# One transformer block on one core: low weight parts on VectorE alone, and two more weight blocks in seven-product form

## The chip, the core and the metric

The kernel runs on one core of a Trainium2 chip. The core has TensorE (PE, with its weight loads PEld), VectorE (DVE), ScalarE (ACT), GpSimd (POOL) and SyncE (SP), each with its own queue that is worked off in order. The metric is the time of one execution on the device in microseconds (us). About 0.5% is what a measurement of this kernel can tell from no change.

## The reference

One layer, a sequence of 512 tokens of width 1024, all in float32. Three sub-layers, each with an RMSNorm before and after, and a residual:

```
proj = rms_norm(x) @ w_in                      # q, k, v for 8 forgetting heads and 8 chunked heads, 8 gates
mix  = [rms(fox_attention), rms(chunk_attention)] @ w_out;   x += rms_norm(mix)
ca   = softmax(h @ w_mem_q @ k_mem.T / 16) @ v_mem @ w_mem_o;  x += rms_norm(ca)     # k_mem, v_mem from mem @ w_mem_kv
h    = rms_norm(x)
g, u = split(h @ w_gate_up)                    # 1024 x 5632
x   += rms_norm((silu(g) * u) @ w_down)        # 2816 x 1024
```

## The kernel before

**Three products for one.** TensorE works on fp32r, a shortened float32. To keep the precision of float32, every operand is split into a high part (the value rounded to fp32r, written by ScalarE) and a low part (the value less its high part). `mm3` issues three matmuls for one product: high by high, high by low, low by high (lines 147 to 149).

**Weights of the first two sub-layers.** `load_unit` (from line 105) brings one unit of weights (w_in, w_out, w_mem_kv, w_mem_q, w_mem_o, the first gate and up blocks) in pieces of 512 KB, tile `raw`, three buffers. For each piece ScalarE writes `hi` (line 124). The low part `lo` is shared out: a number `pk` of the piece's k-blocks goes to GpSimd (line 127), the rest to VectorE (line 131). Of units 256 wide the second piece gives three of its four blocks to GpSimd, so VectorE has 128x256 of it and GpSimd 128x768; of units 18 to 21 (512 wide, w_mem_kv) the second piece goes to GpSimd whole, 128x1024. The first piece of each unit is VectorE's alone. In all GpSimd writes 20 low parts, 16 of 128x768 and 4 of 128x1024. GpSimd also computes the norms' inverse roots (`rstd_of`, line 154, a power), masks and squares.

**The feed-forward part.** Its input columns are cut into 22 blocks of 128: even numbers are gate (G), odd ones up (U). Blocks 0 and 1 come from the units above. A block from 2 on is made in one of two ways. By eight products (`eight`): a 2 by 2 block product as written, 8 products of 4 k-blocks, each three matmuls of 256 columns, 96 matmuls. By seven products (`seven`): a Strassen scheme, 84 matmuls, for which VectorE forms four sums of weight quarters (lines 918 to 921) and puts the output together from the products (lines 1078 to 1088):

```
product(p26[:, left], (h[:, 0], l[:, 0]), b21)
dve.tensor_tensor(out=O[:, 0], in0=halves(p26), in1=twice(v), op=ALU.add)                  # L1078
dve.tensor_tensor(out=O[:, 1, 0], in0=p35[:, left], in1=O[:, 0, 1], op=ALU.add)            # L1079
product(p4[:, left], (h[:, 1], l[:, 1]), t4)
((h, l),) = take()
product(p17[:, right], (h[:, 0], l[:, 0]), t3)
...
product(p35[:, right], (h[:, 1], l[:, 1]), t1)
```

The last product writes into `p35`, the PSUM tile that L1079 reads, so it waits for L1079. An up block has two more VectorE instructions, the products with the gate (L1098, L1100). For the output blocks u = 1 to 3 a further split of the result follows (`keep`, L986 and L987). The tuple `EIGHT` names the blocks that are made by eight products: 2, 3, 8, 13 and 18 of 20.

**The ring.** The weights of these blocks lie in `ring_hi` and `ring_lo`: two single slots of 512 columns and three double slots of 1024. A seven-product block has four items (one single, three doubles), an eight-product block two doubles. A slot is filled again when TensorE has used it: DMA into `fraw` (three buffers), ScalarE writes the high part (L891), VectorE the low part (L892), for items made of sums after the sums.

**What sets the order.** The instructions are put in order, engine by engine, by a list scheduler when the program is built, from priorities (`later`) and its own idea of durations. A change of the work on one engine changes the order on all of them. `w_down` (22 items through the same ring) follows, and with it the last norm.

Of the kernel before, what the change touches and what calls it, by code (L numbers as in the profile page):

```python
# [11 lines left out]
ALU = mybir.AluOpType  # L12
# [24 lines left out]
def hybrid_block_kernel(  # L37
# [20 lines left out]
    act, dve, pool, pe = nc.scalar, nc.vector, nc.gpsimd, nc.tensor  # L58
# [12 lines left out]
    def f32(ap):  # L71
        return ap.bitcast(F32)
# [32 lines left out]
    def load_unit(w, k0, nkb, c0, ncol, dst=None, skip=0):  # L105
        u = len(loaded)
        if dst is None:
            def place(name):
                flat = wp.tile([P, KB * 256 + 48], F32R, tag=name, name=f"{name}{u}", bufs=2)
                return flat[:, skip : skip + nkb * ncol].rearrange("p (k n) -> p k n", k=nkb)  # L110

            hi, lo = place("hi"), place("lo")
        else:
            hi, lo = dst()
        step = nkb if nkb * ncol <= 1024 else 4 if ncol < 512 else 2
        j = 0
        for n in [min(step, nkb - k) for k in range(0, nkb, step)]:
            raw = wp.tile([P, n, ncol], F32, tag="raw", name=f"raw{u}_{j}", bufs=3)
            r0 = (k0 + j) * P
            nc.sync.dma_start(  # L120
                raw,
                w[r0 : r0 + n * P, c0 : c0 + ncol].rearrange("(k p) n -> p k n", p=P),
            )
            act.copy(hi[:, j : j + n, :], raw)  # L124
            pk = 0 if j == 0 or not 0 <= u < 24 else 3 if ncol == 256 else 2 if u >= 18 else 0
            if pk:
                pool.tensor_tensor(  # L127
                    out=lo[:, j : j + pk, :], in0=raw[:, :pk, :], in1=f32(hi[:, j : j + pk, :]), op=ALU.subtract
                )
            if pk < n:  # L130
                dve.tensor_tensor(  # L131
                    out=lo[:, j + pk : j + n, :], in0=raw[:, pk:, :], in1=f32(hi[:, j + pk : j + n, :]), op=ALU.subtract
                )
            j += n
        loaded.append((hi, lo))

# [2 lines left out]
    def unit(ahead=1):  # L139
        n = used[0]  # L140
        used[0] += 1
        while len(loaded) < min(n + 1 + ahead, len(units)):
            load_unit(*units[len(loaded)])
        return loaded[n]
# [63 lines left out]
    for side in range(2):  # L208
        for g in fox_order if side == 0 else (0, 1):
            c = (0, 1544)[side] + 256 * g  # L210
            n = 264 if (side, g) == (0, 1) else 256
# [22 lines left out]
    with tc.tile_pool(name="mix", bufs=1, reuse_waits="tile") as bp:  # L234
# [114 lines left out]
        for t in range(NT):  # L349
# [3 lines left out]
                out=z[:, t, :], in0=acc0[t][:, 256:264], scalar=r, in1=gn[:, B_F : B_F + 8],  # L353
# [284 lines left out]
        with later(-5):  # L638
            for half in range(2):
                hi, lo = unit()  # L640
# [10 lines left out]
    with tc.tile_pool(name="cross", bufs=1, reuse_waits="tile") as cp:  # L651
# [20 lines left out]
        with later(-115):  # L672
            for c in range(4):
                hi, lo = unit()
                acc = bank("a")
                for b in range(2):
# [9 lines left out]
                    out=kT[:, 1, 2 * c : 2 * c + 2, :], in0=a3,  # L686
                    in1=f32(kT[:, 0, 2 * c : 2 * c + 2, :]), op=ALU.subtract,
# [4 lines left out]
        for half in range(2):  # L692
            hi, lo = unit()
            for t in range(NT):
                acc = bank("a")
                for k in range(4):
# [4 lines left out]
                    out=m, in0=acc, scalar=rs_g[1][:, t : t + 1], in1=m, op0=ALU.mult, op1=ALU.add  # L701
# [14 lines left out]
        for half in range(2):  # L716
            accs = [bank("a"), bank("a")]
            for k0 in (0, 4):
                hi, lo = unit()
# [17 lines left out]
        for h in range(4):  # L737
            hi, lo = unit()
            q = qq[:, h % 2]
            for b in range(2):  # L740
                acc = bank("a")
                cs = slice(b * P, (b + 1) * P)
                for k in range(KB):
# [3 lines left out]
                    out=q[:, 1, b, :], in0=acc, scalar=1.0 / 16.0, in1=f32(q[:, 0, b, :]),  # L747
# [3 lines left out]
            for i in range(0, NT, 2):  # L751
                s = bank("s")
                for j in range(2):
# [8 lines left out]
                    out=nm, in_=s.rearrange("p (j n) -> p j n", j=2), axis=AX.X, op=ALU.max, negate=True  # L762
# [8 lines left out]
                for j in range(2):  # L771
                    dve.tensor_scalar(
                        out=p[:, i + j, :], in0=p[:, i + j, :], scalar1=rs[:, j : j + 1],
# [11 lines left out]
            for b in range(2):  # L785
                acc = bank("o")
                cs = slice((2 * h + b) * P, (2 * h + b + 1) * P)
                for k in range(2):
# [6 lines left out]
                    out=oTl[2 * h + b], in0=acc, in1=f32(oTh[2 * h + b]), op=ALU.subtract  # L795
# [27 lines left out]
        for pair in range(2):  # L823
            for half, w in enumerate((w0, w1)):
                for t in (2 * pair, 2 * pair + 1):
                    acc = bank("a")
                    ts = slice(t * P, (t + 1) * P)
                    for k in range(KB):
                        hi, lo = w[k // 4]
# [104 lines left out]
                    fill_from(at, dict(k=4, n=256), lambda k0=k0: load_raw(w_gate_up, k0, 4, c0, 256)),  # L934
                )

        EIGHT = (2, 3, 8, 13, 18)
        for n in range(2, FB):
            (eight_weights if n in EIGHT else seven_weights)(n, (n % 2) * FF + (n // 2) * 256)
        for half in range(2):  # L940
# [28 lines left out]
        def hidden(u):  # L969

            if u == 0:
                return G
            if u < 4:
                return U.rearrange("p t b n -> p b t n")
            if u in (4, 8, 10):
                tag, size = {4: ("vm", 4160), 8: ("pt", 2112), 10: ("up", 2176)}[u]
                gf.append(cp.tile([P, size], F32, tag=tag, name=f"gf{u}"))
            at = (u % 4 if u < 8 else u % 2) * 1024
            return gf[-1][:, at : at + 1024].rearrange("p (b t n) -> p b t n", b=2, t=2)
# [43 lines left out]
        def up_eight(dst):  # L1023
            def done(m, acc):
                dve.tensor_tensor(out=dst[:, m], in0=G[:, :, m], in1=halves(acc), op=ALU.mult)

            return done

        def eight(tags, done):
            accs = [bank(tag) for tag in tags]  # L1030
            for half, bs in enumerate(((b11, b12), (b21, b22))):
                ((h, l),) = take()
                for m in range(2):
                    w = [a[:, :, m * P : (m + 1) * P] for a in (h, l)]
                    for n, ns in enumerate((left, right)):
                        product(accs[m][:, ns], w, bs[n], half == 0 and n == 0, half == 1 and n == 1)
                    if half:
                        done(m, accs[m])
# [67 lines left out]
        for u in range(1, FB // 2):  # L1106
            if 2 * u in EIGHT:
                eight(("a", "a"), gate_eight)
            else:
                seven(G, ("a", "a", "a", "o"), gate_seven)  # L1110
            dst = hidden(u)
            if 2 * u + 1 in EIGHT:
                eight(("s", "s"), up_eight(dst))
# [20 lines left out]
        for half, tail in enumerate((2, 3)):  # L1134
# [17 lines left out]
            for t in range(NT):  # L1152
# [8 lines left out]
                else:  # L1161
# [6 lines left out]
                    for hf in range(2):  # L1168
                        c2 = slice(hf * 512, (hf + 1) * 512)
                        dve.scalar_tensor_tensor(  # L1170
                            out=yd[:, t, c2], in0=yd[:, t, c2], scalar=r, in1=xr[:, t, c2],
# [58 lines left out]
```

## Time and profile before

| what | us |
|---|---|
| median of 3 runs | 801.57 (798.55 to 803.13) |
| the profiled execution, its own time | 796.84 |
| its span, first to last instruction | 795.1 |
| PE busy | 769.5 (97%) |
| VectorE busy | 550.0 (69%) |
| ScalarE busy | 407.2 (51%) |
| GpSimd busy | 117.4 (15%) |

The profiled execution is 4.7 us faster than the median of the runs; durations below are its own. A busy PE is not one at its peak, since matmuls overlap: where matmuls follow one another without a stop, the distance of their starts is what one costs. Idle time in brackets is that of the engine just before the instruction, with the instruction that ended it.

### The profile page before, as it was taken

Reading aid. Unit: us, or ns where it says so; the run is one execution under the profiler, and the core shown is the slowest. Engines: PE = TensorE matmul, PEld = TensorE weight load, DVE = VectorE, ACT = ScalarE, POOL = GpSimd, SP = SyncE. Lnnn points to the kernel's source line nnn. Section 1 sums busy time; section 2 is a strip of 40 time slices with the busy share of each in tenths; the row PEclk is TensorE's granted clock in tenths of the full one; section 3 lists DMA queues with packets and bytes.
Section 4 is the critical chain, followed back from the end, with each engine's and each line's share of the span. In section 5 each row is a group of like instructions: output and inputs, shape, how many; then the busy total and the mean of one; then the engine's idle time right before and its main releaser. Section 6 shows DMA issues by size and latency. Waiting matters only on the chain.

```text
span 795.1 us, 12344 instructions
## 1 busy us (share of the span) xinstructions
PE 769.5 (97%) x4820; PEld 676.5 (85%) x4820; DVE 550.0 (69%) x967; ACT 407.2 (51%) x738; POOL 117.4 (15%) x133
## 2 busy tenths in 40 slices
PE   8998999999999998999999999999999999999996
PEld 8876788887779986778778899999999999888885
DVE  6577988879887578555563779988788878413214
ACT  7357888657786347443552635444434437113111
POOL 6123234220243335200002200000000000000001
PEclk9999999999999999999999999999999999999999
DMA  6341123322312823512351202333243333423202
GB/s 241 85 128 54 54 54 94 105 67 72 116 55 79 300 99 106 158 54 78 102 183 36 80 28 80 107 107 107 80 134 106 107 106 123 138 84 106 101 6 106
DMA packets 60746, 80.02 MB, mean 101 GB/s; under 512 B 2704, under 2 KB 43664, under 8 KB 60688
## 3 DMA queue, kind: packets, MB, share of 16 engines
q1 hardware_dynamic: 59264, 74.49, 29.6%
q0 software_dynamic: 1280, 4.72, 1.7%
q8 instruction: 38, 0.62, 0.3%
q14 instruction: 20, 0.16, 0.1%
q10 hardware_dynamic: 144, 0.02, 0.0%
HBM read 77.13 MB, written 2.10 MB: 100 GB/s over the span
## 4 chain that ended last, share of the span: by engine, by line
PE 74%; DVE 9%; ACT 6%; issue 3%; POOL 2%; DMA 2%; DVEq 0%; POOLq 0%; ACTq 0%
PE ps_a L147 14%; PE ps_a L149 14%; PE ps_a L148 14%; PE ps_s L147 4%; PE ps_s L148 4%; PE ps_s L149 4%; PE ps_t L147 2%; PE ps_t L148 2%; PE ps_t L149 2%; PE ps_t L541 2%; DVE lo L131 2%; DVE ring_lo L892 2%; PE ps_o L147 1%; PE ps_o L550 1%; PE ps_o L148 1%
## 5 line engine op out<-in xcount | busy, mean ns | idle before, releaser
L891 ACT CAST ring_hi<-fraw 128x1024 fp32r<-128x1024 f32 (+1 forms) x62 | 58.4, 946 | 109.0 <-PE ps_o L149 32.4
L892 DVE TENSOR_TENSOR ring_lo<-fraw,ring_hi 128x1024 fp32r<-128x1024 f32 (+1 forms) x62 | 67.7, 1094 | 66.6 <-ACT ring_hi L891 66.5
L131 DVE TENSOR_TENSOR lo<-raw,hi 128x1024 fp32r<-128x1024 f32 (+1 forms) x52 | 67.2, 1300 | 25.4 <-ACT hi L124 25.2
L149 PE MATMUL ps_a<-hTh,lo 128*128 128x512 f32 x192 | 76.0, 396 | 0.6 <-DVE lo L131 0.6
L147 PE MATMUL ps_a<-hTh,hi 128*128 128x512 f32 x192 | 76.5, 398 | 0.2 <-ACT hi L124 0.2
L124 ACT CAST hi<-raw 128x1024 fp32r<-128x1024 f32 x56 | 57.8, 1047 | 36.0 <-PE ps_a L148 14.7
L148 PE MATMUL ps_a<-hTl,hi 128*128 128x512 f32 x192 | 75.5, 393 | 0.0
L127 POOL TENSOR_TENSOR lo<-raw,hi 128x768 fp32r<-128x768 f32 (+1 forms) x20 | 44.8, 2242 | 96.1 <-ACT hi L124 93.1
L891 ACT CAST ring_hi<-sums 128x1024 fp32r<-128x1024 f32 x30 | 31.5, 1050 | 49.1 <-PE ps_a L148 21.7
L147 PE MATMUL ps_a<-b,ring_hi 128*128 128x256 f32 x180 | 49.9, 277 | 0.0
L149 PE MATMUL ps_a<-b,ring_lo 128*128 128x256 f32 x180 | 49.9, 277 | 0.0
L148 PE MATMUL ps_a<-b,ring_hi 128*128 128x256 f32 x180 | 49.9, 277 | 0.0
L892 DVE TENSOR_TENSOR ring_lo<-sums,ring_hi 128x1024 fp32r<-128x1024 f32 x30 | 36.7, 1222 | 11.3 <-ACT ring_hi L891 11.2
L149 PEld LDWEIGHTS ps_a<-hTh,lo 128*128 128x128 f32 x192 | 36.1, 188 | 7.4 <-DVE lo L131 1.0
L147 PEld LDWEIGHTS ps_a<-hTh,hi 128*128 128x128 f32 x192 | 36.1, 188 | 6.3 <-ACT hi L124 0.4
L148 PEld LDWEIGHTS ps_a<-hTl,hi 128*128 128x128 f32 x192 | 36.1, 188 | 6.0
L536 ACT ACTIVATE p<-p,nm 128x128 f32<-128x128 f32 (+1 forms) x64 | 36.1, 564 | 8.4 <-DVE nm L526 7.9
L147 PE MATMUL ps_s<-b,ring_hi 128*128 128x256 f32 x128 | 35.4, 277 | 0.0
L148 PE MATMUL ps_s<-b,ring_hi 128*128 128x256 f32 x128 | 35.4, 277 | 0.0
L149 PE MATMUL ps_s<-b,ring_lo 128*128 128x256 f32 x128 | 35.4, 277 | 0.0
L544 DVE TENSOR_TENSOR ptl<-ps_t,pth 128x128 fp32r<-128x128 f32 (+1 forms) x64 | 30.5, 487 | 7.0 <-ACT pth L543 6.5
L543 ACT CAST pth<-ps_t 128x128 fp32r<-128x128 f32 (+1 forms) x64 | 26.8, 425 | 15.9 <-PE ps_t L541 15.3
(423 smaller groups left out, 2513.6 us busy)
## 6 DMA issues: line engine op xcount, KB each, us to landing
raw<-in_dram SPq DMA_DIRECT2D x64, 512.0 KB, 3.6
fraw<-in_dram SPq DMA_DIRECT2D x62, 512.0 KB, 3.5
cb<-in_dram SPq DMA_DIRECT2D x8, 256.0 KB, 2.6
xo<-in_dram POOLq DMA_DIRECT2D x4, 512.0 KB, 7.4
out_dram<-yd SPq DMA_DIRECT2D x8, 256.0 KB, 2.0
rawv<-in_dram SPq DMA_DIRECT2D x3, 520.0 KB, 6.1
xt<-in_dram SPq DMA_DIRECT2D x3, 512.0 KB, 6.9
gb<-in_dram POOLq DMA_DIRECT2D x3, 512.0 KB, 5.1
```

What stands on the lines that cost most here:

```text
L124: act.copy(hi[:, j : j + n, :], raw)
L127: pool.tensor_tensor(out=lo[:, j : j + pk, :], in0=raw[:, :pk, :], in1=f32(hi[:, j : j + pk, :]), op=ALU.subtract)
L131: dve.tensor_tensor(out=lo[:, j + pk : j + n, :], in0=raw[:, pk:, :], in1=f32(hi[:, j + pk : j + n, :]), op=ALU.subtract)
L147: pe.matmul(dst, sh, mh, start=first, stop=False)
L148: pe.matmul(dst, sh, ml, start=False, stop=False)
L149: pe.matmul(dst, sl, mh, start=False, stop=last)
L536: act.activation(p[:, :n], p[:, :n], AF.Exp, bias=nm, scale=-1.0, accum_out=sm)
L541: pe.transpose(tp[:, k * P : (k + 1) * P], p[:, k * P : (k + 1) * P], ident)
L543: act.copy(span(ph, i), t3)
L544: dve.tensor_tensor(out=span(pl, i), in0=t3, in1=f32(span(ph, i)), op=ALU.subtract)
L891: act.copy(h2, v)
L892: dve.tensor_tensor(out=l2, in0=v, in1=f32(h2), op=ALU.subtract)
```

## The change

The share `pk` is gone: every low part in `load_unit` is one VectorE instruction over the whole piece. `EIGHT` becomes (2, 3, 11): blocks 8, 13 and 18 are made by seven products, block 11 by eight. Blocks made by seven: 17 instead of 15, in runs of 4 to 10 and 12 to 21; before they stood in runs of 4 to 7, 9 to 12, 14 to 17 and 19 to 21. The lines of the changed kernel that follow `load_unit` carry numbers lower by 8.

```
@@ load_unit
             act.copy(hi[:, j : j + n, :], raw)
-            pk = 0 if j == 0 or not 0 <= u < 24 else 3 if ncol == 256 else 2 if u >= 18 else 0
-            if pk:
-                pool.tensor_tensor(
-                    out=lo[:, j : j + pk, :], in0=raw[:, :pk, :], in1=f32(hi[:, j : j + pk, :]), op=ALU.subtract
-                )
-            if pk < n:
-                dve.tensor_tensor(
-                    out=lo[:, j + pk : j + n, :], in0=raw[:, pk:, :], in1=f32(hi[:, j + pk : j + n, :]), op=ALU.subtract
-                )
+            dve.tensor_tensor(out=lo[:, j : j + n, :], in0=raw, in1=f32(hi[:, j : j + n, :]), op=ALU.subtract)
             j += n
...
-        EIGHT = (2, 3, 8, 13, 18)
+        EIGHT = (2, 3, 11)
```

The order, first place: VectorE after the first half of the mixer's output norm, about 296 us in the trace of before. `mix` is the residual stream, `lo` the low part of w_mem_kv, `rs` and `prs` the mean squares that GpSimd turns into inverse roots. Before:

```order
L203 SCALAR_TENSOR_TENSOR mix<-mix,prs_3381,xo_3008 128x1024
L131 TENSOR_TENSOR lo_3523<-raw_0_3524,hi_3522 128x1024
L153 TENSOR_SCALAR rs_3388<-ms_3386 128x1
L153 TENSOR_SCALAR prs_3422<-pms_3420 128x1
L202 TENSOR_TENSOR mix<-mix,gb 128x1024
```

And now:

```order
L195 SCALAR_TENSOR_TENSOR mix<-mix,prs_3367,xo_2997 128x1024
L125 TENSOR_TENSOR lo_3509<-raw_0_3510,hi_3508 128x1024
L125 TENSOR_TENSOR lo_3509<-raw_2_3514,hi_3508 128x1024
L145 TENSOR_SCALAR rs_3374<-ms_3372 128x1
L145 TENSOR_SCALAR prs_3408<-pms_3406 128x1
L194 TENSOR_TENSOR mix<-mix,gb 128x1024
```

The second low part, GpSimd's before, stands in VectorE's queue ahead of `rs`. On TensorE, between the first two transposes of the normed stream and the next six, which need the stream that `rs` scales, stood 26 products with `mT`; now 33 stand there.

Second place: VectorE while TensorE works on block 7 (U) of the feed-forward part. `U` is the output being put together, `sums` and `ring_lo` belong to the weights of blocks 8 and 9. Before, with block 8 by eight products:

```order
L892 TENSOR_TENSOR ring_lo<-fraw_5484,ring_hi 128x1024
L1078 TENSOR_TENSOR U<-ps_s_5441,v 128x512
L1079 TENSOR_TENSOR U<-ps_t_5442,U 128x256
L892 TENSOR_TENSOR ring_lo<-fraw_5514,ring_hi 128x1024
L1084 TENSOR_TENSOR U<-ps_s_5440,U 128x256
L1085 TENSOR_TENSOR U<-ps_t_5443,U 128x256
L918 TENSOR_TENSOR sums<-fraw_5518,fraw_5520 128x512
L1088 TENSOR_TENSOR U<-ps_t_5442,U 128x512
L919 TENSOR_TENSOR sums<-sums,fraw_5518 128x512
L1098 TENSOR_TENSOR U<-G,U 128x2x256
L1100 SCALAR_TENSOR_TENSOR U<-G,U 128x2x256
L920 TENSOR_TENSOR sums<-sums,fraw_5520 128x512
```

And now, with block 8 by seven:

```order
L884 TENSOR_TENSOR ring_lo<-fraw_5548,ring_hi 128x512
L910 TENSOR_TENSOR sums<-fraw_5548,fraw_5550 128x512
L884 TENSOR_TENSOR ring_lo<-sums,ring_hi 128x1024
L1070 TENSOR_TENSOR U<-ps_s_5425,v 128x512
L911 TENSOR_TENSOR sums<-sums,fraw_5548 128x512
L1071 TENSOR_TENSOR U<-ps_t_5426,U 128x256
L884 TENSOR_TENSOR ring_lo<-fraw_5433,ring_hi 128x4x2x128
L1076 TENSOR_TENSOR U<-ps_s_5424,U 128x256
L912 TENSOR_TENSOR sums<-sums,fraw_5550 128x512
L1077 TENSOR_TENSOR U<-ps_t_5427,U 128x256
L1080 TENSOR_TENSOR U<-ps_t_5426,U 128x512
L884 TENSOR_TENSOR ring_lo<-sums,ring_hi 128x1024
```

A sum for the block after next now stands between L1070 and L1071 (L1078 and L1079 before), the instruction for which TensorE's last product of the block waits, and the items of block 8 are made of sums.

## Rows read from the trace of the kernel before

**Rows 1.** The page's busy time, share of the span and instructions of each engine.

```profile
PE 769.5 (97%) x4820; PEld 676.5 (85%) x4820; DVE 550.0 (69%) x967; ACT 407.2 (51%) x738; POOL 117.4 (15%) x133
```

**Rows 2.** The low part on VectorE: durations in ns, least, median, most; both shapes.

```profile
L131 DVE TENSOR_TENSOR lo<-raw,hi x52: 409/1225/3016, 34.4 to 393.6; 128x1024 fp32r<-128x1024 f32 x36, 128x256 fp32r<-128x256 f32 x16
```

**Rows 3.** Groups by shape, VectorE: busy us, mean ns, idle before.

```profile
L131 DVE TENSOR_TENSOR lo<-raw,hi 128x256 fp32r<-128x256 f32 x16 | 19.6, 1227 | 0.1
...
L918 DVE TENSOR_TENSOR sums<-fraw,fraw 128x512 f32<-128x512 f32 x15 | 10.3, 687 | 0.8 <-DMA fraw<-in_dram 0.7
```

**Rows 4.** Groups by shape, GpSimd, 36 to 337 us.

```profile
L127 POOL TENSOR_TENSOR lo<-raw,hi 128x768 fp32r<-128x768 f32 x16 | 33.6, 2098 | 76.0 <-ACT hi L124 73.1 <-DVE fd L450 3.0
L127 POOL TENSOR_TENSOR lo<-raw,hi 128x1024 fp32r<-128x1024 f32 x4 | 11.3, 2819 | 20.1 <-ACT hi L124 20.1
```

**Rows 5.** Timeline near 109 us: start, duration, engine, instruction.

```profile
109.01 1.83 POOL L127 TENSOR_TENSOR lo<-raw,hi 128x768 fp32r<-128x768 f32 x1 [6.41 <-ACT hi L124]
109.34 1.65 DVE L538 TENSOR_SCALAR p<-p,rc 128x256 f32<-128x256 f32 x1
```

**Rows 6.** Timeline of TensorE: the idle gaps that the prediction names.

```profile
64.25 0.49 PE L487 MATMUL ps_s<-c,sel 128*128 128x512 f32 x1 [0.88 <-DVE c L467]
...
111.13 0.30 PE L541 MATMUL ps_t<-ident,p 128*128 128x128 f32 x1 [1.16 <-DVE p L538]
...
159.29 0.38 PE L147 MATMUL ps_a<-hi,hTh 128*128 128x256 f32 x1 [1.14 <-DVE V L342]
...
176.75 0.30 PE L541 MATMUL ps_t<-ident,p 128*128 128x128 f32 x1 [0.94 <-DVE p L538]
...
319.15 0.50 PE L148 MATMUL ps_a<-lo,mT 128*128 128x512 f32 x1 [0.99 <-DVE lo L131]
```

**Rows 7.** Timeline from 296 us, the engines one after another.

```profile
296.15 3.80 POOL L127 TENSOR_TENSOR lo<-raw,hi 128x1024 fp32r<-128x1024 f32 x1 [1.07 <-ACT hi L124]
...
297.75 0.15 DVE L153 TENSOR_SCALAR rs<-ms 128x1 f32<-128x1 f32 x1
...
299.91 1.52 POOL L154 TENSOR_TENSOR rs<-rs,mhalf 128x1 f32<-128x1 f32 x1
...
301.47 1.15 ACT L162 ACTIVATE xo<-mix,rs 128x1024 f32<-128x1024 f32 x1 [2.71 <-POOL rs L154]
...
302.67 0.47 PE L173 MATMUL ps_t<-ident,xo 128*128 128x128 f32 x1 [2.74 <-ACT xo L162]
...
316.08 3.02 DVE L131 TENSOR_TENSOR lo<-raw,hi 128x1024 fp32r<-128x1024 f32 x1
```

**Rows 8.** Busy time by stretch: us, PE, PEld, DVE, ACT, POOL, then granted clock, DMA.

```profile
299.90:302.70 2.80, 0.06 (x2) 0.04 (x1) 1.84 (x2) 1.23 (x2) 2.05 (x3) 0.92 0.43 132
302.70:306.00 3.30, 3.30 (x12) 2.88 (x13) 2.30 (x4) 3.08 (x6) 0.00 (x0) 0.55 0.54 205
```

**Rows 9.** Timeline of TensorE: first matmul of blocks 4, 12 and 14.

```profile
490.65 0.28 PE L147 MATMUL ps_a<-b,ring_hi 128*128 128x256 f32 x1
...
570.90 0.28 PE L147 MATMUL ps_a<-b,ring_hi 128*128 128x256 f32 x1
...
591.30 0.28 PE L147 MATMUL ps_a<-b,ring_hi 128*128 128x256 f32 x1
```

**Rows 10.** Whom TensorE waited for, 440 to 680 us: total, times, longest.

```profile
PE ps_a L147 <- DVE G L1079: 0.7, 2, 0.4
```

**Rows 11.** Timeline of VectorE: L1079 of blocks 4, 5, 9, 10, and one wait.

```profile
498.89 0.42 DVE L1079 TENSOR_TENSOR G<-ps_a,G 128x256 f32<-128x256 f32 x1
...
508.46 0.42 DVE L1079 TENSOR_TENSOR U<-ps_t,U 128x256 f32<-128x256 f32 x1
...
542.55 1.23 DVE L892 TENSOR_TENSOR ring_lo<-sums,ring_hi 128x1024 fp32r<-128x1024 f32 x1 [1.86 <-ACT ring_hi L891]
...
549.30 0.42 DVE L1079 TENSOR_TENSOR U<-ps_t,U 128x256 f32<-128x256 f32 x1
...
559.53 0.42 DVE L1079 TENSOR_TENSOR G<-ps_a,G 128x256 f32<-128x256 f32 x1
```

## Prediction, made before the changed kernel was run

> **What bounds the kernel now.** I read the busy times first: TensorE is busy 97% of the span, VectorE 69%, GpSimd 15% [rows 1]. So a change is worth what it does to TensorE: matmuls that go, and stops that go or come. Then I read the groups by shape for the low parts, the timeline of TensorE for its stops, and what stood on VectorE and GpSimd just before each.
>
> The low part on VectorE takes 1.22 us for 128x1024, and 0.41 us at best for 128x256 [rows 2]. Yet the sixteen of 128x256 that have a GpSimd partner average 1.23 us [rows 3]: as long as the whole piece. The partner of 128x768 takes 2.10 us on GpSimd [rows 4]. Beside it other VectorE instructions that read SBUF are held too: a 128x256 scaling at 109.34 takes 1.65 us and ends when GpSimd's 109.01 + 1.83 does [rows 5]. So VectorE pays for GpSimd's share in waiting.
>
> TensorE's stops lie there. Outside the feed-forward part the larger ones are 0.88 us at 64.25, 1.16 at 111.13, 1.14 at 159.29, 0.94 at 176.75 and 0.99 at 319.15, all ended by VectorE [rows 6]. The largest is 2.74 us at 302.67: `rs` is ready on VectorE at 297.90, but GpSimd is in a low part of 3.80 us until 299.95, and only then computes the root; ScalarE scales at 301.47, and TensorE gets its operand [rows 7]. After this stop the granted clock is 0.55 of full for 3.3 us [rows 8], that is, mostly the lower of its two levels, 1.2 instead of 2.4 GHz.
>
> In the feed-forward part TensorE is the pace. Blocks 12 (seven products, 84 matmuls) and 13 (eight, 96) take 591.30 - 570.90 = 20.40 us, 0.1133 us each [rows 9]: 9.52 us for a block by seven, 10.88 by eight. Blocks 4 to 11, seven by seven products and one by eight, should take 7 x 9.52 + 10.88 = 77.5 us, and take 80.25 [rows 9]: 2.7 us lost, of which 0.7 is named as a wait for L1079 on VectorE [rows 10]. The rest I can't name.
>
> **The change part by part.** *Low parts on VectorE alone.* Added to VectorE: 16 x (1.225 - 0.409) = 13.1 us for the wider pieces and 4 x 1.22 = 4.9 for the new ones, 18.0 in all. Taken from it: the excess of the sixteen, 16 x (1.227 - 0.409) = 13.1 [rows 2, 3], and the holding of other instructions, 1.3 us each at the place shown [rows 5]. So VectorE's time comes out about even. The end depends on the places.
>
> The Trainium skill speaks to both sides here (Perfetto Trace Analysis, section Optimizing Scalar/DVE Operations): if VectorE is saturated, moving work even to GpSimd may make sense, but the two share a port to SBUF, so it might not help. Taken by its first half, undoing such a move would put 18 us back on VectorE; the trace agrees with its second half, 1227 against 409 ns.
>
> At 296 to 320 us: `rs` now has two low parts ahead of it on VectorE instead of one, so it is ready 1.22 us later, at 299.1. The root takes up to 1.52 us, ScalarE started 0.04 us after it and TensorE 1.20 us after that [rows 7]: 299.1 + 1.5 + 0.04 + 1.2 = 301.9. TensorE has 33 products ahead instead of 26, seven more of 0.23 us (twice a 256-column matmul), so it runs until 299.9 + 1.6 = 301.5. The stop falls from 2.74 to 0.4: -2.3 us. Without it the clock should not fall; what the lower clock cost was 3.3 x (1 - 0.55) = 1.5 us [rows 8]. The low part at 316.08 takes 3.02 us instead of 1.22 [rows 7] and stops TensorE at 319.15; of that 0.99 us I take 0.8. Sum -4.6; bounds -5.4 (all three whole: 2.74 + 1.5 + 0.99, and little beside) and -1.0 (only the last).
>
> In the attention part, to 250 us, the four gaps sum to 4.1 us [rows 6], and each has a held VectorE instruction before it. They can go. But ten of the wider pieces lie there, each 0.82 us longer in VectorE's queue than an unhindered 128x256, ahead of softmax steps; TensorE stopped for VectorE at four of ten such places, so I let four tenths of 8.2 us come back, 3.3. Sum -0.8. Bounds: -4.1, nothing comes back; +4.1, all 8.2 come back. The new order of all engines is in this range too.
>
> *Two blocks more by seven products.* TensorE: 2 x 12 matmuls fewer, 24 x 0.1133 = -2.7 us.
>
> VectorE: four sums of 0.69 us [rows 3] for each more, and the putting together. What decides is the run length. From L1079 of one block to that of the next VectorE took 508.46 - 498.89 = 9.57 us from a gate to an up block, and 559.53 - 549.30 = 10.23 from up to gate, where the products with the gate come in [rows 11]. TensorE needs 9.52. In a run of sevens VectorE is later by 0.05 and 0.71 us by turns, and once it is late TensorE waits at the last product of each block. After an eight-product block VectorE catches up, since that asks neither sums nor putting together; before there was one for every four, now one after seven.
> Run 4 to 10: steps 4 to 5, 5 to 6, 6 to 7, 7 to 8 count (after that no sums stand ahead, block 11 being by eight). They cost 9.57, 10.23, 9.57, 10.23, with two instructions of `keep` (1.22 each), and two sums fewer by the new order (0.69 each): 40.66 against 4 x 9.52 = 38.08, +2.6. The longest wait named, 0.4, falls in block 4 [rows 10] and stays: +0.4.
> Run 12 to 21: seven steps until 19 (from then on no sums for a block after): 4 x 9.57 + 3 x 10.23 = 68.97 against 66.64, +2.3.
> New loss 5.3 us; it stands for the 2.7 of before. So +2.6, and with the matmuls -0.1: this half is worth nothing. Bounds: -5.4, no waits at all (2.7 matmuls and 2.7 old loss); the other end below, as a rival.
>
> Sum: -4.6 - 0.8 - 0.1 = -5.5 us. Against the profiled execution's 796.84 this is 791.3; the runs' median lies 4.7 us above that execution, and against it I predict 801.57 - 5.5 = **796.1 us**.
>
> **The rivals.** *TensorE alone counts in the feed-forward part.* VectorE's two periods together, 19.80 us, are only 4% over TensorE's 19.04, and they may hold short waits that shrink when it is late; then it stays level: 801.57 - 4.6 - 0.8 - 5.4 = 790.8. For it: blocks 12 and 13 ran with no loss. Against it: the wait for L1079 is there even in runs of four.
> The Trainium skill has this as a rule (Perfetto Trace Analysis, section Identifying the Most-Contended Engine): the engine with the highest occupancy is to be optimised first. TensorE is that one, and by the rule the 24 matmuls are a plain gain.
>
> *VectorE waits as well as TensorE (the slower side).* When TensorE is late, it frees ring slots late, ScalarE's cast comes late, and VectorE stands idle before its low part: 1.86 us at 542.55 [rows 11]. Place: the two runs of sevens, 11 steps, 5.5 pairs. If one such wait falls in each pair, +10.2: 796.1 + 10.2 = 806.3. It decides from 5.5 / 5.5 = 1.0 us per pair on (slower than before), and from (5.5 + 4.0) / 5.5 = 1.7 on beyond what can be told. Against it: in the two periods measured VectorE waited for nothing so long.
>
> *The attention part takes the gain back.* All 8.2 us come back: +4.1 instead of -0.8, 801.0. For it: VectorE is TensorE's releaser at every gap there. Against: the held instructions go.
>
> That the change doesn't do what it says: GpSimd keeps the roots, masks and squares, and these may still hold VectorE; they are shorter, and I count them as unchanged.
>
> **How the numbers follow.** Forecast 0.54, with its own range 792 to 800; TensorE alone 0.12; VectorE waits too 0.14; attention takes it back 0.20. Faster by over 0.5% means below 797.6, slower above 805.6. The forecast falls below 797.6 in two thirds of its cases, 0.36; with 0.12 and a little of the attention case, 0.02, faster is 0.50. Slower: 0.11 of the waiting case and 0.03 of the attention case, 0.14. The rest, 0.36, is the same. The range, 789.5 to 805, takes in three cases whole and leaves out most of the slower one.
>
> **What would show it.** After: no low part on VectorE over 1.3 us; no stop of over 1 us before the transposes near 302 and full clock behind it; GpSimd's root within 1.6 us after `rs`. Feed-forward: waits for L1071 (L1079 before) near blocks 5 to 9 and 13 to 19, some 0.4 us per block, none in 10 and 11. Wrong would be: stops of TensorE before 250 us that sum to more than before; a mean distance of over 10.8 us from one L1071 to the next in the runs (the waiting rival); or no waits at all in the runs of sevens.

## The result and the profile after

The changed kernel takes 795.45 us (median of 6 runs, 794.01 to 796.44), the kernel before 801.92 us (6 runs, 798.55 to 803.13): ratio 0.9922, 95% interval 0.9901 to 0.9943. Predicted were 796.1 us. In the first set of experiments the ratio of the same two kernels was 0.9956 (0.9938 to 0.9973). So the change is worth 3.5 to 6.5 us, by the two sets. Three executions of this case took 948, 1544 and 2700 us, and the ratios leave them out. The total came out as predicted; where it comes from did not.

The two profiled executions, 796.84 and 795.24 us, are only 1.6 us apart. One execution varies more than that, for two reasons told below; so a part of the change is measured here between fixed points of the traces, and the whole by medians.

The page's busy times after, for [rows 1], and the low part on VectorE, for [rows 2]:

```profile
PE 769.0 (97%) x4796; PEld 676.6 (85%) x4796; DVE 555.2 (70%) x993; ACT 411.6 (52%) x748; POOL 73.6 (9%) x113
```

```profile
L125 DVE TENSOR_TENSOR lo<-raw,hi x56: 1186/1220/1486, 34.6 to 390.2; 128x1024 fp32r<-128x1024 f32 x56
```

The holding is gone: VectorE took over all of GpSimd's share, and its busy time rose by 5.2 us only. The longest low part is 1.49 us, where 3.02 stood [rows 2]; I had asked for 1.3, and this one, at 214.87 us, lies beside two of the squares that GpSimd keeps (`msq`, 1.30 and 1.28 us). TensorE has 24 matmuls less, but its busy time fell by 0.5 us, not by 2.7.

TensorE's largest stops from 40 to 250 us after, for the first four of [rows 6] (timeline: start, duration, instruction, idle time before it and what ended it):

```profile
68.60 0.50 PE L514 MATMUL ps_s<-T,Q 128*128 128x512 f32 x1 [1.22 <-DVE nm L518]
...
105.77 0.39 PE L514 MATMUL ps_s<-T,Q 128*128 128x256 f32 x1 [0.68 <-ACT fb L484]
...
156.88 0.39 PE L139 MATMUL ps_a<-hi,hTh 128*128 128x256 f32 x1 [0.53 <-DVE V L334]
...
203.97 0.33 PE L533 MATMUL ps_t<-ident,p 128*128 128x128 f32 x1 [0.65 <-DVE p L530]
...
245.25 0.38 PE L139 MATMUL ps_a<-mT,hi 128*128 128x256 f32 x1 [1.02 <-ACT hi L124]
```

The stops at 64, 111 and 177 us are gone, and the one at 159 is half as long. The largest now stood before as well, where the prediction did not list it:

```profile
69.01 0.50 PE L522 MATMUL ps_s<-T,Q 128*128 128x512 f32 x1 [1.10 <-DVE nm L526]
```

New are 0.68 us at 105.77 and 1.02 us at 245.25, both ended by ScalarE. All idle stretches of TensorE over 0.15 us between 25 and 250 us sum to 9.5 us before and 7.1 after; those ended by VectorE fall from 7.9 to 4.1, those ended by ScalarE rise from 0.6 to 2.1.

Around 300 us, for [rows 7]: the first stop of the norm's transposes, and what stands behind it.

```profile
300.48 0.88 PE L165 MATMUL ps_t<-ident,xo 128*128 128x128 f32 x6 [0.23 <-ACT xo L154]
...
306.76 1.22 DVE L194 TENSOR_TENSOR mix<-mix,gb 128x1024 f32<-128x1024 f32 x1
...
306.92 1.46 POOL L146 TENSOR_TENSOR prs<-prs,mhalf 128x1 f32<-128x1 f32 x1 [2.46 <-DVE prs L145]
...
308.41 1.28 DVE L195 SCALAR_TENSOR_TENSOR mix<-mix,prs,xo 128x1024 f32<-128x1024 f32 x1
...
309.62 0.87 DVE L178 SCALAR_TENSOR_TENSOR hTl<-ps_t,gn,hTh 128x256 fp32r<-128x256 f32 x2
...
310.63 0.30 PE L165 MATMUL ps_t<-ident,xo 128*128 128x128 f32 x1 [1.58 <-DVE hTl L178]
```

The 2.74 us stop shrank to 0.23, even below the 0.4 forecast. But ten microseconds later TensorE stops 1.58 us, which before did not happen. The chain behind that stop is VectorE's: GpSimd's next root lasts 1.46 us beside L194, a VectorE instruction with two SBUF operands, so L195 cannot start until 308.41, and the turned operand `hTl` is queued behind L195. L194 itself ends at 307.98, so the long root accounts for 0.4 us of the stop; for the rest, TensorE came there earlier than VectorE could follow.

Two more stops came ahead of it, which before had no counterpart:

```profile
268.61 1.05 ACT L124 CAST hi<-raw 128x1024 fp32r<-128x1024 f32 x1 [4.06 <-DMA raw<-in_dram]
...
270.98 0.50 PE L140 MATMUL ps_a<-lo,oh 128*128 128x512 f32 x1 [0.76 <-DVE lo L125]
...
292.30 0.44 PE L165 MATMUL ps_t<-ident,xo 128*128 128x128 f32 x2 [0.85 <-DVE prs L145]
```

At 270.98 TensorE waits for a low part of VectorE, and this one for weights that had only just landed: ScalarE's cast had waited 4.06 us for them. From 250 to 340 us the stops of TensorE over 0.08 us sum to 4.3 us before and 3.6 after.

And the low clock moved along. Busy time by stretch after, for [rows 8] (us, then busy time and instructions of PE, PEld, DVE, ACT, POOL, then granted clock, DMA share, GB/s):

```profile
302.00:306.00 4.00, 4.00 (x22) 3.16 (x21) 3.74 (x8) 4.00 (x9) 0.54 (x1) 1.00 0.22 72
311.90:315.40 3.50, 3.50 (x13) 2.97 (x13) 2.55 (x4) 0.51 (x2) 0.00 (x0) 0.51 0.06 11
```

Behind the new stop the granted clock is 0.51 for 3.5 us, TensorE's lower level of 1.2 GHz.

In the third stage the waits for VectorE, for [rows 10] (487 to 668 us; waited in total, times, longest), and the largest with what VectorE did before it:

```profile
PE ps_a L139 <- DVE G L1071: 1.5, 5, 0.4
PE ps_t L139 <- DVE U L1071: 1.4, 1, 1.4
```

```profile
523.61 0.69 DVE L910 TENSOR_TENSOR sums<-fraw,fraw 128x512 f32<-128x512 f32 x1 [1.68 <-DMA fraw<-in_dram]
...
526.55 0.42 DVE L1071 TENSOR_TENSOR U<-ps_t,U 128x256 f32<-128x256 f32 x1
```

```profile
527.03 0.38 PE L139 MATMUL ps_t<-thi,ring_hi 128*128 128x256 f32 x1 [1.37 <-DVE U L1071]
```

They are named waits of 2.9 us for 0.7 before. The largest is in block 7: VectorE stood 1.68 us idle for weights from DRAM, and then ran without a stop until L1071. In this trace, the changed kernel's second one and that of eight blocks alone (both below) that idle time is 1.68, 1.57 and 1.05 us and the wait 1.37, 1.28 and 0.66.

### The profile page after: what moved, and what is told of

It is laid out like the page before. It is cut to its first block, busy times and chain, and to the rows that moved or that the text cites. A ratio compares the mean times of both kernels' runs of the same rounds, so it can differ in the third digit from the quotient of the medians.

```text
span 793.2 us, 12301 instructions
## 1 busy us (share of the span) xinstructions
PE 769.0 (97%) x4796; PEld 676.6 (85%) x4796; DVE 555.2 (70%) x993; ACT 411.6 (52%) x748; POOL 73.6 (9%) x113
## 4 chain that ended last, share of the span: by engine, by line
PE 49%; DVE 7%; issue 3%; ACT 1%; DMA 1%; POOL 0%; DVEq 0%; POOLq 0%; ACTq 0%
PE ps_a L139 8%; PE ps_a L140 8%; PE ps_a L141 8%; PE ps_s L139 4%; PE ps_s L140 4%; PE ps_s L141 4%; DVE ring_lo L884 3%; PE ps_t L139 2%; PE ps_t L140 2%; PE ps_t L141 2%; PE ps_o L139 1%; PE ps_o L140 1%; PE ps_o L141 1%; PE ps_t L165 1%; ACT ring_hi L883 1%
## 5 line engine op out<-in xcount | busy, mean ns | idle before, releaser
L125 DVE TENSOR_TENSOR lo<-raw,hi 128x1024 fp32r<-128x1024 f32 x56 | 67.9, 1224 | 25.9 <-ACT hi L124 25.7
L883 ACT CAST ring_hi<-sums 128x1024 fp32r<-128x1024 f32 x34 | 35.7, 1050 | 56.3 <-PE ps_a L140 24.4
L884 DVE TENSOR_TENSOR ring_lo<-sums,ring_hi 128x1024 fp32r<-128x1024 f32 x34 | 41.5, 1222 | 4.5 <-ACT ring_hi L883 4.3
L139 PE MATMUL ps_a<-b,ring_hi 128*128 128x256 f32 x140 | 38.9, 278 | 0.0
L141 PE MATMUL ps_a<-b,ring_lo 128*128 128x256 f32 x140 | 38.8, 277 | 0.0
L140 PE MATMUL ps_a<-b,ring_hi 128*128 128x256 f32 x140 | 38.8, 277 | 0.0
L533 PE MATMUL ps_t<-ident,p 128*128 128x128 f32 x160 | 28.1, 275 | 1.1 <-DVE p L530 0.8
```

The costliest lines, as they stand in the source:

```text
L125: dve.tensor_tensor(out=lo[:, j : j + n, :], in0=raw, in1=f32(hi[:, j : j + n, :]), op=ALU.subtract)
L139: pe.matmul(dst, sh, mh, start=first, stop=False)
L140: pe.matmul(dst, sh, ml, start=False, stop=False)
L141: pe.matmul(dst, sl, mh, start=False, stop=last)
L533: pe.transpose(tp[:, k * P : (k + 1) * P], p[:, k * P : (k + 1) * P], ident)
L883: act.copy(h2, v)
```

## The experiments

Three sets of four kernels, each set on one chip, on which the kernel before ran as well: 33 runs with a median of 799.24 us beside the first set, 30 with 798.43 beside the second, 17 with 801.57 beside the third. The ratios are to these runs, with 95% intervals, and are not quotients of the medians.

**The two parts apart.** Both kernels again, and each part of the change alone.

```
low parts alone:    dve.tensor_tensor over the whole piece;  EIGHT = (2, 3, 8, 13, 18)
eight blocks alone: pk as before;                            EIGHT = (2, 3, 11)
```

The kernel before. 

> The kernel before, unchanged, to have its profile beside the others on one chip. If the first profiled execution of before (796.84 us) was an unusually quick one, this one shows 800 to 803 us, and block 4 of the third stage starts later than at 490.65 us; if the quick one was typical of profiled executions, it shows 796 to 798 us again, and the median of its timed runs stays near 801.9.

Low parts alone. 

> All low parts by VectorE, but 18 gate and up blocks' choice left as before (2, 3, 8, 13, 18 by eight products). My sum gives the low parts -5.4 us (T1 and T2) and nothing to the blocks, less what VectorE's longer queue costs: about 796.5 us, ratio 0.993. Rival one, all gain is in the low parts and the blocks cost a little (the traces: 3.3 us gained ahead of block 4, 1.4 lost behind it): about 794 us, faster than the whole change. Rival two, the low parts give nothing: 801 to 802 us.

Eight blocks alone. 

> GpSimd keeps its share of the low parts; blocks by eight products are 2, 3, 11 instead of 2, 3, 8, 13, 18. My sum: matmuls -2.7, waits of TensorE for VectorE's last product operand +2.6, so 801.8 us, ratio 1.000. Rival one (the blocks cost 1 to 2 us, as the two traces from block 4 to 21 have it): 803 us. Rival two (the blocks carry the gain, 24 matmuls fewer and waits hidden): 799 us.

The changed kernel. 

> The changed kernel again, on the chip of the three others: 795.5 us and ratio 0.992 if medians are what counts. If its gain is made up of two independent parts, its difference to before equals the sum of those of the two kernels with one part each, within 1 us; my sum says -5.4 and -0.1.

Measured: before 801.05 us, profiled 797.97, ratio 1.0012 (0.9983 to 1.0041); low parts alone 794.55, ratio 0.9938 (0.9917 to 0.9960); eight blocks alone 799.19, 1.0000 (0.9983 to 1.0018); both 796.35, 0.9956 (0.9938 to 0.9973). All of the gain is the low parts', as forecast, and the other half is worth nothing by itself, also as forecast. Beside the low parts it may cost something: the parts' gains sum to 5.0 us and the whole gains 3.5, 1.5 apart where within 1 was expected; but the intervals overlap. The rival by which the 24 matmuls count in full, 2.7 us or a ratio of 0.9966, lies outside the interval of eight blocks alone.

VectorE's busy time shows the holding in one number. The page of low parts alone, for [rows 1]:

```profile
PE 768.6 (97%) x4820; PEld 676.7 (85%) x4820; DVE 543.0 (69%) x971; ACT 407.0 (51%) x738; POOL 73.6 (9%) x113
```

VectorE does GpSimd's 20 pieces besides its own, and is busy 7.0 us less than before (550.0). In eight blocks alone it is busy 563.0, 13.0 more.

**Which low parts.** Before, GpSimd had 14 pieces of 128x768 up to 267 us, and six pieces (two of 128x768, four of 128x1024) from 286 to 332 us. One kernel gives VectorE the early ones, one the late ones.

```
-pk = 0 if j == 0 or not 0 <= u < 24 else 3 if ncol == 256 else 2 if u >= 18 else 0
+pk = 0 if j == 0 or not 18 <= u < 24 else 3 if ncol == 256 else 2      # early ones to VectorE
+pk = 0 if j == 0 or not 0 <= u < 18 else 3 if ncol == 256 else 0       # late ones to VectorE
```

Early ones. 

> VectorE takes the 14 early low parts (128x768, 37 to 267 us), GpSimd keeps the six late ones (286 to 332 us). My prediction put 4.6 of its 5.4 us on the late ones, so this would be 798.5 us, ratio 0.999. The aligned traces of the kernel with all on VectorE show the rival: 2.6 us gained by 166 us, 3.0 by 250, 3.3 by the end of the first two stages; then this one is 795.5 to 796.5 us, ratio 0.995 to 0.996.

Late ones. 

> The complement: GpSimd keeps the 14 early low parts, VectorE takes the six late ones. My prediction: 4.6 us of gain, 795.3 us, ratio 0.994. The rival from the aligned traces: 0.3 us of gain or none, 799 us, ratio 1.000, since the stop of 2.7 us at 300 us is replaced by one of 1.6 us ten microseconds later and the half clock comes with it.

Measured: 797.11 us, ratio 0.9988 (0.9969 to 1.0007), and 796.93 us, 0.9981 (0.9962 to 1.0000). Neither alone can be told from no change with certainty, and the times don't choose between the two theories: by the ratios the halves gain 1.0 and 1.5 us, together less than low parts alone, but the intervals leave room for it. The traces choose, between fixed points. The first point is the end of TensorE's pause near 36 us, the second its first product with `ones` and `sq`. The kernel before (its second trace), low parts alone, early ones, late ones:

```profile
37.45 0.50 PE L149 MATMUL ps_a<-hTh,lo 128*128 128x512 f32 x1 [0.59 <-DVE lo L131]
...
165.70 0.95 PE L575 MATMUL ps_t<-ones,sq 128*128 128x1 f32 x8
```

```profile
35.98 0.50 PE L141 MATMUL ps_a<-hTh,lo 128*128 128x512 f32 x1 [0.59 <-DVE lo L125]
...
161.60 0.95 PE L567 MATMUL ps_t<-ones,sq 128*128 128x1 f32 x8
```

```profile
36.01 0.50 PE L149 MATMUL ps_a<-hTh,lo 128*128 128x512 f32 x1 [0.60 <-DVE lo L131]
...
161.38 0.95 PE L575 MATMUL ps_t<-ones,sq 128*128 128x1 f32 x8
```

```profile
37.59 0.50 PE L149 MATMUL ps_a<-hTh,lo 128*128 128x512 f32 x1 [0.59 <-DVE lo L131]
...
165.76 0.94 PE L575 MATMUL ps_t<-ones,sq 128*128 128x1 f32 x8
```

From the one to the other it takes 128.2, 125.6, 125.4 and 128.2 us. Over all 14 traces of this case this distance is 128.1 to 128.2 in the four with GpSimd's early share, and 125.3 to 125.6 in the nine without (the one left over is the next experiment). So some 2.7 us are gained in the first 165 us, and in either group this distance repeats within 0.3 us. The table has the same for a later point, the first product of `kT` and `qq`, near 335 us.

| kernel | pause to `ones,sq` | pause to `kT,qq` | clock 0.5 near 300 to 320 us | slow matmuls | span |
|---|---|---|---|---|---|
| before, first trace | 128.1 | 301.2 | yes | 292 | 795.1 |
| before, again | 128.2 | 300.9 | yes | 27 | 796.2 |
| eight blocks alone | 128.1 | 301.2 | yes | 382 | 796.2 |
| late ones on VectorE | 128.2 | 298.7 | no | 21 | 794.9 |
| early ones on VectorE | 125.4 | 298.7 | yes | 543 | 794.8 |
| low parts alone | 125.6 | 297.6 | yes | 445 | 792.4 |
| low parts alone, again | 125.5 | 295.7 | no | 346 | 791.9 |
| changed, first trace | 125.4 | 297.5 | yes | 372 | 793.2 |
| changed, again | 125.5 | 296.2 | no | 606 | 792.7 |

(Slow matmuls: those from 456 to 671 us that start 0.1155 to 0.123 us after the one before, where others take 0.1133; counts to within 4.) With the clock low in both, low parts alone gain 3.3 to 3.6 us by 335 us, 2.5 of them by 165. With the clock full, all low parts on VectorE gain 4.7 to 5.6. The late ones by themselves gain 2.2 to 2.5 us by then, with the clock full: half of the 4.6 predicted, and far more than the rival's 0.3.

**GpSimd's work without its use.** Low parts alone, and GpSimd subtracts a tile from itself where its share stood, 11 times in the first 240 us; nobody reads the result.

```
...
+            if j and ncol == 256 and idle:
+                same = f32(hi[:, j : j + 3, :])
+                pool.tensor_tensor(out=idle[0], in0=same, in1=same, op=ALU.subtract)
...
```

> All low parts on VectorE, eight blocks' choice as before; GpSimd runs beside them, in the first 240 us, 11 operations of 128x768 that subtract a tile from itself into a tile that nobody reads (they stand where GpSimd's own share stood, the tiles that VectorE needs are not touched by them). If VectorE is held by GpSimd's operations themselves, its low parts grow beside them (over 1.3 us) and TensorE is at its first transpose near 162 us about 1 to 3 us later than without them (counted from TensorE's pause near 36 us): span 1 to 3 us longer. If the gain came only from GpSimd no longer delivering its own share late, nothing moves: VectorE's low parts stay at 1.22 us and the 162 us point stays within 0.3 us.

Measured: 798.75 us, ratio 0.9983 (0.9958 to 1.0007), where low parts alone beside it have 0.9923 (0.9897 to 0.9950). The two fixed points:

```profile
36.06 0.50 PE L145 MATMUL ps_a<-hTh,lo 128*128 128x512 f32 x1 [0.60 <-DVE lo L126]
...
164.29 0.95 PE L572 MATMUL ps_t<-ones,sq 128*128 128x1 f32 x8
```

That is 128.2 us: the gain of the early part is gone. That it is gone to the last tenth is chance, since VectorE does more here than before; by the first product of `mT` with a low part this kernel is 1.2 us behind the kernel before (214.5 us against 213.2 and 213.4). The low parts of VectorE, 25 to 250 us, with and without (busy us, mean ns):

```profile
L126 DVE TENSOR_TENSOR lo<-raw,hi 128x1024 fp32r<-128x1024 f32 x26 | 36.6, 1413 | 1.6 <-ACT hi L125 1.5
```

```profile
L125 DVE TENSOR_TENSOR lo<-raw,hi 128x1024 fp32r<-128x1024 f32 x28 | 34.2, 1226 | 1.8 <-ACT hi L124 1.6
```

And one place of it near 177 us, with its counterpart in low parts alone below:

```profile
175.53 1.47 POOL L129 TENSOR_TENSOR idle<-hi 128x768 bf16<-128x768 f32 x1 [2.50 <-ACT hi L125]
...
175.87 1.28 DVE L535 TENSOR_SCALAR p<-p,rc 128x256 f32<-128x256 f32 x1
...
177.30 0.41 PE L538 MATMUL ps_t<-ident,p 128*128 128x128 f32 x2 [0.59 <-DVE p L535]
```

```profile
173.18 0.35 DVE L530 TENSOR_SCALAR p<-p,rc 128x256 f32<-128x256 f32 x1
...
173.86 0.38 PE L533 MATMUL ps_t<-ident,p 128*128 128x128 f32 x2
```

VectorE's scaling takes 1.28 us beside GpSimd's operation and 0.35 without, and TensorE stops for it. So GpSimd's operation as such brings the time back, not a low part delivered late. One rival is left: its 21 us also stand ahead of GpSimd's own masks and squares, which could come late. Of TensorE's eight stops over 0.55 us between 60 and 240 us, seven are ended by VectorE and one by ScalarE, none by GpSimd; and the one wait of any engine for GpSimd from 36 to 250 us is the same with the idle work and without:

```profile
ACT msq L604 <- POOL msq L606: 0.3, 1, 0.3
```

```profile
ACT msq L599 <- POOL msq L601: 0.3, 1, 0.3
```

So its masks and squares did not come late for anyone, and the holding is what remains.

**The wait for L1071.** The last product of a block of seven goes to the half bank that L1070 frees, one VectorE operation earlier.

```
-            product(p35[:, right], (h[:, 1], l[:, 1]), t1)
-            dve.tensor_tensor(out=O[:, 1], in0=twice(p35[:, right]), in1=O[:, 1], op=ALU.add)
+            product(p26[:, left], (h[:, 1], l[:, 1]), t1)
+            dve.tensor_tensor(out=O[:, 1], in0=twice(p26[:, left]), in1=O[:, 1], op=ALU.add)
```

On the changed kernel. 

> The changed kernel, with the last product of a seven block written into the bank that VectorE's operation of L1070 frees, not into that of L1071. The traces of the changed kernel name L1071 as what TensorE waits for in the third stage (2.1 to 2.9 us in all, 1.3 of it in block 7); L1071 ends 0.9 us behind L1070 there. If that wait is what the fewer eight blocks cost, it falls to under 1 us and the kernel takes 794.5 us where the changed one takes 796.3, ratio to before 0.994. Rival: the wait moves to the next operand of VectorE (a ring_lo or ps bank) and the time stays at 796.

On low parts alone. 

> Low parts on VectorE alone, blocks by eight products as before (2, 3, 8, 13, 18), and the last product in the bank of L1070. There is only 0.4 us of waiting left in the third stage of that kernel without the new bank, so 794.2 us, ratio 0.994, the same as without it. Rival: a bank that is taken earlier makes later work wait, 795 to 796 us.

Measured: 793.56 us, ratio 0.9940 (0.9919 to 0.9961), and 797.42 us, 0.9975 (0.9955 to 0.9995), though the second's profiled execution took 790.08, the shortest of all; 794.5 and 794.2 were expected. In the first kernel the waits fall to 1.5 us, not to under 1, and are now for L1070, in blocks 7 and 8:

```profile
PE ps_s L139 <- DVE U L1070: 0.8, 1, 0.8
PE ps_a L139 <- DVE G L1070: 0.7, 1, 0.7
```

**Three kernels again.**

Low parts alone with the new bank. 

> The kernel with low parts on VectorE, eight blocks' choice as before and the bank of L1070, once more: its one profile showed 790.1 us and its other eleven runs 795 to 799. If the TensorE pace of 0.118 us instead of 0.113 us per matmul takes it, this profile shows long stretches of that pace when it reads above 795 us, and few when it reads near 790. If its slow runs have another cause, stalls that the first profile did not show stand in this one.

Low parts alone. 

> Low parts on VectorE alone, once more: 794.5 us, ratio 0.994, if its lead over the changed kernel is more than chance. If a profile's time is only chance of pace and half clock, it is 793 to 797 us.

Changed with the new bank. 

> The changed kernel with the bank of L1070, once more: 793.6 us, ratio 0.994, the best candidate beside the one with low parts on VectorE alone. If it is no better than the changed kernel, ratio 0.9955.

Measured: 795.04 us, ratio 0.9907 (0.9871 to 0.9943); 794.77, 0.9923 (0.9897 to 0.9950); 794.15, 0.9903 (0.9876 to 0.9929). The ratio of one kernel moves by up to 0.7% from one set to the next (0.9975 and 0.9907), so of the four kernels without GpSimd's share none is shown to be better than another. Low parts alone (0.9938 and 0.9923) and changed with the new bank (0.9940 and 0.9903) lie a little below the changed kernel (0.9956 and 0.9922), within the intervals.

## Why the prediction was right, and where it was not

**The holding** was right. It is gone, and GpSimd's idle work alone brings it back. The Trainium skill (Perfetto Trace Analysis, section Optimizing Scalar/DVE Operations) warns that VectorE and GpSimd share a port to SBUF, so that moving work between them might not help; the 0.35 and 1.28 us agree, and here it even cost.

**The attention part, predicted -0.8, measured -3.0** (pause to the first product of `mT` with a low part: 213.18 us before, 210.14 in the first trace of the changed kernel; 213.36 and 210.31 in before, again, and low parts alone). The step "four tenths of 8.2 us come back" was wrong. Before 250 us no new stop over 0.35 us is ended by VectorE, though it has the wider pieces in its queue; what new stops there are wait for ScalarE. (The pieces there are 11, not ten.) Of the -4.1 that goes, 3.6 went.

**The stretch from 296 to 320 us, predicted -4.6, measured -0.6 in the two first traces, counted from 250 us on** (of the 3.7 us by the `kT,qq` point 3.0 lie ahead of 250). The terms that I listed came: the stop of 2.74 us fell to 0.23, as worked out, and the 0.99 at 319 went with the low part of 3.02 us. But "what is late next" was not asked. TensorE, earlier now, stopped 1.58 us at 310.63, by VectorE and GpSimd's second root, and 0.76 and 0.85 us at 270.98 and 292.30: 3.2 us, a term that the sum had at nothing. The clock: "without it the clock should not fall" was wrong as put, since the new stop can bring it as well. It fell in all 4 traces with GpSimd's late share, behind 2.74 to 2.78 us, and in 3 of 10 without it (changed, low parts alone, idle work), behind 1.58 or 1.59. The step of -1.5 was about right in size: traces of one kernel with the clock low and full differ by 1.3 us (changed) and 2.0 (low parts alone) at the `kT,qq` point. But whether it comes is a matter of chance; at these frequencies, 4 of 4 and 3 of 10, it is 0.7 x 1.5 = -1.0 on the mean, and so few traces leave that rough.

**The third stage, predicted -0.1, measured nothing** (ratio 1.0000). Its two halves are there. From the first matmul of block 4 to the last of block 21 the traces have every matmul, 1548 with five blocks by eight and 1524 with three. This stretch, less 0.1133 us for each and less what the slow pace adds (last section), is what stops cost: 4.5, 5.2 and 4.5 us in the three traces with three blocks by eight and the old bank (eight blocks alone, changed twice), and 1.0 to 2.4, mean 1.8, in the seven with five. So 2.9 us of stops came for 2.7 us of matmuls. I had 5.3 for 2.7: the new sum nearly right, the old one too large, and the difference of 2.6 right by that much luck. Of the 2.7 us between blocks 4 and 12 of which I could name 0.7, about 1.2 is no stop but the slow pace, from 519 to 550 us.
The lagging VectorE is right where nothing disturbs it: the seven steps of L1071 from block 12 to block 19 take 69.02 us in the first trace, predicted 68.97. But the named waits stand in blocks 4, 6, 7, 8, 14 and 16, not in each block from 5 to 9 and 13 to 19, and the largest comes of weights that VectorE waits for, which the rule has not. The Trainium skill's rule that the engine of highest occupancy comes first (Perfetto Trace Analysis, section Identifying the Most-Contended Engine) did not decide here: 24 matmuls off the busiest engine gave no time.

**The sum.** -3.0 in the attention, -0.6 behind it, -1.0 for the odds of the clock and 0 in the third stage make -4.6, where the ratios show -3.5 to -6.5. That the total of -5.5 was right is luck: a term 3 us too large (296 to 320) stood beside one 2.2 us too small (attention).

**Rivals.** That attention takes the gain back is refuted. That VectorE waits too is refuted as a size: in the 11 steps it waits over 1 us once, 1.68 us, not once in each of 5.5 pairs, and from one L1071 to the next in the two runs it takes 9.9 and 9.8 us on the mean, below the 10.8 that were to show it. That TensorE alone counts is not borne out.

**Still open:** why the profiled execution of before was 4.7 us quicker than the median of its runs. Before, again, lay at 797.97 beside a median of 801.05; the clock and pace below move a run by as much, but the timed runs leave no rows to show it.

## What to carry to other kernels

Work that was moved to GpSimd was not free here, since VectorE was held beside it: look for VectorE instructions whose longest is several times their shortest, and give GpSimd none of that work before any finer step. When a stop is taken away, follow the engines that the next operands come from for some ten microseconds, since TensorE now comes earlier to all of them; here three new stops took back 3.2 us. And where runs vary by more than the change, measure a part between two fixed instructions of the trace; here that repeated within 0.3 us, where the ratio of one kernel moved by 0.7% (some 5 us) from one set to the next.

## What was not expected of the hardware

TensorE has two paces at full granted clock. One kernel (low parts alone with the new bank) was traced twice, 788.1 and 795.2 us long. Busy time by stretch, TensorE (us, busy and matmuls, granted clock, DMA share, GB/s), first the quick trace:

```profile
486.00:536.00 50.00, 50.00 (x442) 1.00 0.34 106
536.00:586.00 50.00, 49.78 (x437) 1.00 0.37 116
586.00:636.00 50.00, 50.00 (x444) 1.00 0.33 106
```

```profile
486.00:536.00 50.00, 50.00 (x427) 1.00 0.31 95
536.00:586.00 50.00, 50.00 (x427) 1.00 0.36 107
586.00:636.00 50.00, 50.00 (x427) 1.00 0.34 106
```

Some 440 against 427 matmuls in 50 us, clock 1.00 in both, and the slow trace has no stop. Each matmul is 0.1178 us behind the last instead of 0.1133, for 1787 of them, 8.0 us in all; the quick trace has stops of 0.9 us in blocks 4 to 21 that the slow one has not, and the spans differ by 7.1. The slow pace began near 458.6 us here, near 506.1 in low parts alone, and there it ended where two matmuls stood 0.25 us apart, at 557.3. It comes with every version of the kernel and in no fixed place. What starts it was not found.

GpSimd's root of 128x1 takes 0.54 us where no L194 runs beside it (the POOL column of the stretch from 302 to 306 us above), and 1.46 beside L194 of VectorE, at 306.92: the holding works in both directions.

The low clock does not follow from the stop alone: after the same stop of 1.58 us the changed kernel's second trace had it full.

```profile
311.33 0.30 PE L165 MATMUL ps_t<-ident,xo 128*128 128x128 f32 x1 [1.58 <-DVE hTl L178]
```

```profile
311.90:315.40 3.50, 3.50 (x19) 2.96 (x20) 3.44 (x6) 1.14 (x4) 0.54 (x1) 1.00 0.02 5
```
